# A DiT block on one core: the unused tile in front of the left-hand activations, 64 bytes in place of 192

## The chip, the cores and the metric

The kernel runs on one core of a Trainium2 chip. The metric is the device time of one execution in microseconds; the time before is the median of three runs. The profile is one execution of the same program, recorded instruction by instruction.

## The reference, cut to what matters

One block of a diffusion transformer over 256 latent and 256 context tokens, all in float32:

```
mod = silu(c) @ w_ada + b_ada                      # shift, scale, gate, twice
h   = modulate(rmsnorm(x))                         # latent and context
z   = h @ w_in      # differential attention q k v, MLA compressions, two gates
o_a, o_b = two attentions of 8 heads (latent queries, all keys)
x   = x + g1 * ((sigmoid(ga) * (o_a @ w_o_da) + sigmoid(gb) * (o_b @ w_o_mla)) @ w_out)
x   = x + g2 * ((silu(h2 @ w_gate) * (h2 @ w_up)) @ w_down)   # hidden size 5632
out = rmsnorm(x)                                   # model size 2048
```

The change leaves all of it as it is.

## The kernel before, in words

Activations lie in SBUF with the features on the partitions and the tokens in the free dimension. Every weight matrix is streamed once from HBM, in units of up to 512 KB: `load_w` (L161) puts a unit of 128 x 1024 values into one of five `raw` buffers, and `split_w` makes two parts of it, a rounded part `wh` (ScalarE copy, L169) and the rest `wl` (VectorE subtraction, L170), each with three buffers. The activations are kept as such a pair too. A product is three matmuls: rounded weights with both parts of the activations, and the weights' rest with the rounded activations.

Nearly all matmuls are issued by `Acc.mm` (L155 is the first of a PSUM bank, L157 all others). `GroupT` loads a 128x128 piece of the weights into the array and streams 256 tokens of an activation (gate, up, ga, gb, yab, wo, cq and others). `group_b` does it the other way round: it loads 128 tokens of an activation and streams the weights, 256 columns for dv and 512 for the down projection. A gate or up group is 512 features, 8 units of two k-tiles, 192 matmuls; there are 11 of each, in turn. In groups 2 to 6 a background generator, `gemv` (L495 to L512), multiplies a row of `w_ada` on VectorE into `gacc` at each tick, and after 16 of them its sink issues four matmuls into `gs` (L932 and L933) with 512 columns. The order on TensorE is the program's order; a matmul waits for its unit's split, and the split for its load and for a free buffer.

SBUF tiles come from two stacks. Pools without a side are laid one behind the other from low addresses, pools with `side="right"` from the top downwards. The low stack is `const`, then `stream` (wl, wh, raw), then `apart`, which holds one tile, `gap`, that nothing reads or writes, and then the left-hand pools: kvp, tp, oT, kp, oTbp, qp, yp, xtp, h2p, op, gp and dp. A tile's room is rounded up to 32 bytes in each partition. The program's layout before, in bytes of a partition, with the remainder by 512:

| tiles | first address | remainder |
|---|---|---|
| wl, wh, raw (stream) | 25,120, 37,408, 49,696 (last raw ends at 70,176) | 32 |
| ckvn, x2k (left) | 70,368 | 224 |
| h (left; moving operand of gate and up) | 86,752 and 103,136 | 224 |
| ph, pl (left) | 93,920 and 102,112 | 224 |
| oTa, oTb, cqn, dk, kn (left) | 110,560, 126,944, 143,328, 126,944, 151,520 | 480 |
| hl, hc and mT (right) | 196,576 and 163,808 | 480 |
| hid (right; loaded operand of down) | 130,336 and 175,392 | 288 |

The right-hand pool of the feed-forward part has an unused tile of its own, `hgap`, of 192 bytes, which the change leaves.

Of the kernel before, what the change touches and what calls it, by code (L numbers as in the profile page):

```python
# [11 lines left out]
F32 = mybir.dt.float32  # L12
# [6 lines left out]
P = 128  # L19
# [77 lines left out]
def kernel(  # L97
# [9 lines left out]
    def pool(name, bufs=1, space=None, side=None):  # L107
        st = ExitStack()
        kw = {}
        if space is not None:  # L110
            kw["space"] = space
        if side is not None:
            kw["side"] = side
        pl = st.enter_context(tc.tile_pool(name=name, bufs=bufs, reuse_waits="tile", **kw))
        return pl, st.close
# [5 lines left out]

    apart, _c3 = pool("apart")
    ctx.callback(_c3)
    apart.tile([P, 48], F32, name="gap")
    pacc, _c2 = pool("pacc", space=PSUM)
    ctx.callback(_c2)

# [909 lines left out]
```

## Time and profile before

| | |
|---|---|
| median of three runs | 1593.17 us (1586.82 to 1597.92) |
| the profiled execution | 1590.97 us |
| its span, first to last instruction | 1589.2 us |
| TensorE busy with matmuls | 1536.9 us (97%) |
| VectorE, ScalarE, GpSimd busy | 1015.8, 736.8, 16.1 us |
| read from HBM | 352.37 MB, 223 GB/s over the span |

Busy time of TensorE counts each matmul to its modelled end, and matmuls overlap, so it doesn't say how fast they follow each other. In the chain of waits, a piece such as "PE up L157 x187" is a row of matmuls that follow each other, and its length is the sum of their distances from start to start. Some matmul records are missing from a trace, so a count can be short by a little.

### The profile page before, as it was taken

How to read it: one execution, taken by the hardware profiler on the slowest of the kernel's cores; microseconds unless marked ns; L12 is line 12 of the kernel's file. 1: busy time of each engine (PE TensorE's matmuls, PEld its weight loads, DVE VectorE, ACT ScalarE, POOL GpSimd, SP SyncE). 2: the span in 40 equal slices, each digit the busy share in tenths (PEclk: the TensorE clock that was granted, in tenths of full speed). 3: DMA queues.
4: the chain of work that ended last, by engine and by line, in shares of the span. 5: the costliest groups of instructions: out<-in, count | busy, mean ns of one | idle time of the engine just before them, and what ended most of it. 6: DMA issues, size and time to landing. Idle time of an engine off the chain costs nothing.

```text
span 1589.2 us, 28863 instructions
## 1 busy us (share of the span) xinstructions
PE 1536.9 (97%) x11966; PEld 1443.3 (91%) x11966; DVE 1015.8 (64%) x1360; ACT 736.8 (46%) x1038; POOL 16.1 (1%) x14
## 2 busy tenths in 40 slices
PE   3899999998999999999999999999999999999997
PEld 2678899998899999999999999999999999888886
DVE  5437887787896667677777566767555545455454
ACT  4335455545675444444446444444444444344343
POOL 0000000000000000000000000000000000011010
PEclk9999999999999999999999999999999999999999
DMA  9894653456454787878884668888566656665563
GB/s 369 338 366 161 210 176 111 139 176 202 150 160 162 258 280 259 291 266 296 299 280 148 229 226 300 289 271 280 196 191 196 197 192 220 194 192 197 191 193 120
DMA packets 100595, 356.34 MB, mean 224 GB/s; under 512 B 10993, under 2 KB 13553, under 8 KB 100209
## 3 DMA queue, kind: packets, MB, share of 16 engines
q1 hardware_dynamic: 99600, 351.58, 65.9%
q10 hardware_dynamic: 864, 2.93, 0.5%
q8 instruction: 93, 1.52, 0.4%
q14 instruction: 38, 0.30, 0.1%
HBM read 352.37 MB, written 2.10 MB: 223 GB/s over the span
## 4 chain that ended last, share of the span: by engine, by line
PE 72%; DMA 9%; DVE 6%; issue 1%; ACT 1%; DVEq 0%; POOLq 0%; POOL 0%; ACTq 0%
PE gate L157 15%; PE up L157 15%; PE down L157 15%; DMA raw<-in_w_ada_dram 9%; PE ga L157 4%; PE dv L157 4%; PE gb L157 3%; DVE gacc L507 3%; PE dk L157 2%; DVE wl L170 2%; PE yab L157 2%; PE wo L157 2%; PE dq L157 1%; PE cq L157 1%; PE pt L647 1%
## 5 line engine op out<-in xcount | busy, mean ns | idle before, releaser
L170 DVE TENSOR_TENSOR wl<-raw,wh 128x1024 fp32r<-128x1024 f32 (+1 forms) x453 | 548.9, 1222 | 326.9 <-ACT wh L169 312.6
L169 ACT CAST wh<-raw 128x1024 fp32r<-128x1024 f32 (+1 forms) x453 | 474.9, 1051 | 572.7 <-PE down L157 134.9
L507 DVE SCALAR_TENSOR_TENSOR gacc<-raw,cols,gacc 128x1024 f32<-128x1024 f32 x120 | 154.0, 1283 | 123.5 <-DMA raw<-in_w_ada_dram 123.2
L157 PE MATMUL gate<-h,wh 128*128 128x256 f32 x1386 | 175.9, 277 | 0.0
L157 PE MATMUL up<-h,wh 128*128 128x256 f32 x1386 | 175.8, 277 | 0.0
L157 PE MATMUL down<-wh,hid 128*128 128x512 f32 x696 | 173.3, 389 | 0.0
L157 PEld LDWEIGHTS up<-h,wh 128*128 128x128 f32 x1386 | 166.4, 188 | 0.1
L157 PEld LDWEIGHTS gate<-h,wh 128*128 128x128 f32 x1386 | 166.5, 188 | 0.0
L157 PEld LDWEIGHTS down<-wh,hid 128*128 128x128 f32 x696 | 130.7, 188 | 27.0
L157 PE MATMUL gate<-h,wl 128*128 128x256 f32 x704 | 96.7, 277 | 0.0
L157 PE MATMUL up<-h,wl 128*128 128x256 f32 x704 | 96.7, 277 | 0.0
L157 PE MATMUL down<-wl,hid 128*128 128x512 f32 x352 | 94.6, 389 | 0.0
L157 PEld LDWEIGHTS up<-h,wl 128*128 128x128 f32 x704 | 87.8, 188 | 0.2 <-DVE wl L170 0.2
L157 PEld LDWEIGHTS gate<-h,wl 128*128 128x128 f32 x704 | 87.8, 188 | 0.1
L157 PEld LDWEIGHTS down<-wl,hid 128*128 128x128 f32 x352 | 66.1, 188 | 13.7
L157 PE MATMUL ga<-hl,wh 128*128 128x256 f32 x504 | 65.6, 278 | 0.0
L157 PE MATMUL wo<-mT,wh 128*128 128x256 f32 x504 | 64.2, 278 | 0.0
L157 PE MATMUL gb<-hl,wh 128*128 128x256 f32 x504 | 64.0, 278 | 0.0
L157 PEld LDWEIGHTS ga<-hl,wh 128*128 128x128 f32 x504 | 61.4, 188 | 0.6 <-ACT wh L169 0.4
L157 PEld LDWEIGHTS wo<-mT,wh 128*128 128x128 f32 x504 | 60.6, 188 | 0.4 <-issue 0.4
L157 PEld LDWEIGHTS gb<-hl,wh 128*128 128x128 f32 x504 | 60.7, 188 | 0.0
L408 PE MATMUL pgb<-sraw,c 128*32 128x512 f32 (+1 forms) x288 | 32.8, 597 | 17.4 <-DMA sraw<-in_w_mod_dram 17.4
(334 smaller groups left out, 2316.5 us busy)
## 6 DMA issues: line engine op xcount, KB each, us to landing
raw<-in_w_ada_dram SPq DMA_DIRECT2D x128, 512.0 KB, 4.2
raw<-in_w_in_dram SPq DMA_DIRECT2D x119, 512.0 KB, 4.6
raw<-in_w_ffn_gate_dram SPq DMA_DIRECT2D x88, 512.0 KB, 4.4
raw<-in_w_ffn_up_dram SPq DMA_DIRECT2D x88, 512.0 KB, 4.4
raw<-in_w_ffn_down_dram SPq DMA_DIRECT2D x88, 512.0 KB, 3.6
sraw<-in_w_mod_dram SPq DMA_DIRECT2D x64, 512.0 KB, 8.5
raw<-in_w_out_dram SPq DMA_DIRECT2D x32, 512.0 KB, 5.1
raw<-in_w_o_da_dram SPq DMA_DIRECT2D x16, 512.0 KB, 4.8
```

The source lines that it names most:

```text
L157: nc.tensor.matmul(region, lhsT, rhs, start=False, stop=last, skip_group_check=key != self.lead)
L169: nc.scalar.copy(h, v)
L170: nc.vector.tensor_sub(l, v, h.bitcast(F32))
L408: nc.tensor.matmul(pgb[32 * j : 32 * j + 32, :w], c32[:, kt, :], vs[kt], start=kt < 4, stop=kt >= 12, tile_position=(0, 32 * j))
L507: nc.vector.scalar_tensor_tensor(a, raw, cols[:, kt : kt + 1], a, op0=ALU.mult, op1=ALU.add)
L647: nc.tensor.transpose(pt[:, j * P : (j + 1) * P], a[:, j * P : (j + 1) * P], ident)
```

## The change

The unused tile `gap` gets 16 float32 values in each partition in place of 48, 64 bytes in place of 192.

```diff
     apart, _c3 = pool("apart")
     ctx.callback(_c3)
-    apart.tile([P, 48], F32, name="gap")
+    apart.tile([P, 16], F32, name="gap")
     pacc, _c2 = pool("pacc", space=PSUM)
     ctx.callback(_c2)
```

## Rows read from the trace of the kernel before

**Rows 1.** The page, busy time of each engine.
```profile
PE 1536.9 (97%) x11966; PEld 1443.3 (91%) x11966; DVE 1015.8 (64%) x1360; ACT 736.8 (46%) x1038; POOL 16.1 (1%) x14
```
**Rows 2.** The chain of waits in time, feed-forward part: start us, us, what.
```profile
965.89 21.19 PE up L157 x187
987.65 21.20 PE gate L157 x187
1010.35 22.02 PE up L157 x187
...
1078.19 22.02 PE gate L157 x187
1101.72 21.19 PE up L157 x187
...
1341.20 59.16 PE down L157 x261
```
**Rows 3.** Windows, TensorE: from:to, us, busy (matmuls), granted clock, DMA share, GB/s.
```profile
493.30:542.40 49.10, 49.10 (x419) 1.00 0.75 254
...
629.20:638.30 9.10, 9.10 (x79) 1.00 0.76 245
...
785.30:807.70 22.40, 22.40 (x192) 1.00 0.88 314
...
1009.60:1100.00 90.40, 90.40 (x769) 1.00 0.83 281
1101.10:1340.30 239.20, 239.20 (x2113) 1.00 0.60 196
```
**Rows 4.** The chain of waits in time, other stages.
```profile
215.76 16.84 PE dv L157 x143
...
276.69 21.19 PE dv L157 x187
...
509.38 22.02 PE gb L157 x187
531.99 10.72 PE yab L157 x91
544.06 4.88 PE yab L157 x43
```
**Rows 5.** The timeline at 1008 us, TensorE from gate over gs to up.
```profile
1008.23 0.62 PE L157 MATMUL gate<-h,wl 128*128 128x256 f32 x4
...
1008.68 0.39 PE L932 MATMUL gs<-wh,ones_r 128*128 128x512 f32 x1
...
1009.60 0.28 PE L155 MATMUL up<-h,wh 128*128 128x256 f32 x1
```
**Rows 6.** Groups by line and shape: busy us, mean ns of one, then idle before.
```profile
L170 DVE TENSOR_TENSOR wl<-raw,wh 128x1024 fp32r<-128x1024 f32 x451 | 547.6, 1224 | 324.6 <-ACT wh L169 312.6 <-PE dv L157 6.3 <-PE gs L521 3.0
...
L157 PE MATMUL gate<-h,wh 128*128 128x256 f32 x1386 | 175.9, 277 | 0.0
...
L548 DVE TENSOR_TENSOR pl<-pt,ph 128x512 fp32r<-128x512 f32 x32 | 21.9, 687 | 3.9 <-ACT ph L547 3.5
...
L548 DVE TENSOR_TENSOR hid<-s,hid 128x512 fp32r<-128x512 f32 x22 | 15.1, 688 | 4.8 <-ACT hid L547 4.8
...
L659 PE MATMUL po<-ph,mv 128*128 128x256 f32 x32 | 9.6, 299 | 0.0
...
L548 DVE TENSOR_TENSOR mT<-ga,mT 128x512 fp32r<-128x512 f32 x8 | 5.2, 686 | 0.0
```
**Rows 7.** DMA issues into left-hand tiles: count, KB each, median us to landing.
```profile
x2T<-in_xt_dram SPq DMA_DIRECT2D x4, 512.0 KB, 6.5
...
fgb<-in_final_norm_g_dram ACTq DMA_DIRECT2D x1, 1024.0 KB, 7.5
```
**Rows 8.** The timeline from 128 to 142 us: last modulation matmuls, first temporary.
```profile
128.63 3.64 PE L408 MATMUL pgb<-sraw,c 128*32 128x512 f32 x32
...
141.31 0.44 DVE L555 STREAM_SHUFFLE r<-g 128x256 f32<-128x256 f32 x1
```
**Rows 9.** Windows over other stretches of long spacing, columns as in rows 3.
```profile
215.90:232.40 16.50, 16.50 (x142) 1.00 0.57 171
...
39.30:41.20 1.90, 1.90 (x18) 1.00 1.00 395
...
133.80:148.90 15.10, 15.10 (x130) 1.00 0.35 106
...
856.00:867.30 11.30, 11.30 (x97) 1.00 0.01 1
```

## The prediction
> **What bounds the kernel now.** I read the page's busy shares first, then the chain of waits in order of time, then windows over TensorE's long stretches, and last the groups by line and shape. TensorE is busy 1536.9 of 1589.2 us, VectorE 1015.8, ScalarE 736.8 [rows 1]. The two feed-forward projections, gate and up, fill the span from 855 us to 1340 us and the down projection the rest; in all of it the chain runs on TensorE from group to group with no piece of another engine between them [rows 2]. So what counts is how far one matmul starts behind the one before it, and that can be read from the chain, since a piece of 187 matmuls in sequence lasts 187 spacings.
>
> There are two spacings for the same shape. Most gate and up groups take 21.19 or 21.20 us for 187, 113.3 ns each; four groups in a row, from 1010 to 1100 us, take 22.02 us, 117.8 ns each [rows 2]. The granted clock is 1.00 (the level of 2.4 GHz) in both, so it isn't the clock [rows 3]. The same two spacings are met outside that stage: dv 21.19 us for 187 and 16.84 for 143 (117.8), gb 22.02 for 187, yab 10.72 for 91 (117.8) and 4.88 for 43 (113.5) [rows 4]. The down projection, with 512 columns, takes 59.16 us for 261, 226.7 ns, which is twice 113.3 [rows 2]. The switch comes where another kind of matmul stands between: the gate group that ends at 1008.7 us is followed by four 512-column matmuls into gs, and the up group behind them begins at 117.8 ns [rows 5]; behind the next four gs matmuls, at 1100.2 us, the pieces are short again [rows 2]. No address differs between the gate groups on either side. A spacing, once taken up, is held until the next break.
>
> **The change, part by part.** It removes 128 bytes of a tile that nothing reads or writes: no instruction, no DMA and no wait goes or comes, and the order on every queue stays. What it does is to lower the start of every left-hand tile allocated behind the gap by 128 bytes in each partition. By the positions in the kernel's description, h goes from 224 to 96 past a multiple of 512, and the weights stay at 32: its distance to them goes from 192 to 64. For oTa, oTb, cqn and the dk and kn tiles the distance goes from 448 to 320. Between two left-hand tiles nothing changes, and right-hand tiles (hl, hc, mT, hid) keep theirs.
>
> Step 1, VectorE and ScalarE: VectorE's 128x512 subtraction takes 688 ns into hid (288 past a multiple of 512), 686 into mT (480) and 687 into pl (224) [rows 6]. Three positions, one duration within 2 ns; 2 ns on the 32 writes of pl are under 0.1 us either way, beside TensorE's work. The costly split, 1224 ns times 451, touches only the weights' pool, which doesn't move [rows 6]. I take 0.
>
> Step 2, DMAs: the weights' buffers don't move. The loads into moved tiles are four of x2T, 6.5 us from issue to landing, and one of final_g, 7.5 us [rows 7]. Each x2T load lies beside a w_out group of TensorE and only has to land before that group's end. If that cover were gone, the four would cost 26 us; nothing in the change takes it. I take 0.
>
> Step 3, buffer reuse: the moved tiles overlap slightly other parts of the closed right-hand pools. The modulation weights (sraw) are last read at 132.3 us and the first left-hand temporary (r) is written at 141.3 us [rows 8], so a wait that comes or goes there is over 9 us early. I take 0; the bounds are nothing gained and, with that cover gone, 9 us once.
>
> Step 4, TensorE, the only step with a real unknown: does the distance between the streamed operand and the loaded one set the spacing? The rows of before contain the new distance already. In dv the streamed operand is wh (32) and the loaded one hl or hc (480), so the streamed one lies 64 past the other, counted round 512, just as h will lie to wh in gate and up. There the two spacings are 113.3 and 117.8 ns, no other [rows 4]. And at the distance of 448 (gb, and yab) the same two are seen [rows 4], as at 192 in gate and up [rows 2]. So I expect the same two spacings afterwards, and the break, not the address, to choose which. The cost of the step is then what the choice falls on.
>
> The price of the choice: 117.8 less 113.3 is 4.5 ns a matmul. The stretches of long spacing that last over some 140 matmuls and the one of 79 at 629 us hold 419, 79, 192, 769 and, in dv, 142 matmuls; twelve short ones, of 18 to 130, hold 569 more (97 of them at 856 us) [rows 3, 9]: 2,170 in all, so about 9.7 us of this execution. If all of them went, 1590.97 us would become 1581.3. Should the one long stretch of 2,113 matmuls from 1101 us [rows 3] begin at the other spacing, it would cost 2,113 times 4.5 ns, 9.5 us. The three runs of before lie 11.1 us apart (1586.82 to 1597.92), which is what one or two such stretches are worth. I take the expected change of step 4 as zero, with 8 us to either side.
>
> Sum: 0 + 0 + 0 + 0 on the profiled execution of 1590.97 us (span 1589.2 and 1.8 around it). That execution is 2.2 us under the median of the runs shown, 1593.17. I put the forecast between them: 1592 us, no change, with a range of its own from 1584 to 1600.
>
> **The rivals.** About 1% is what a measurement of this kernel can tell from no change: under 1577.2 or over 1609.1 us.
>
> A, slower: at the distances 64 and 320 the left-hand stages fall into the long spacing at each restart. Place: gate and up first, 4,224 matmuls of which 769 and 97 have it already; 3,358 times 4.5 ns is 15.1 us. yab has 768, some 100 long already: 3.0 us. cq and the latent-attention projections have some 300 left: 1.3 us. Together 19.4 us, 1610 us. It decides from the point where more than 4,000 matmuls take up the long spacing. A third, longer one is not excluded by the few hundred dv matmuls: 6 ns beyond the short one in place of 4.5 would make it 1616. The far end is the row of po, which streams ph at 299 ns a matmul against gate's 277 [rows 6]; 22 ns on 4,224 matmuls would be 93 us and 1684, but those stand in short runs behind waits, so it is no estimate. For A: nothing else that could set the rhythm changes here, and both spacings are a coin's toss now, so a bias could be large. Against: dv held the short one for 187 in a row at that distance.
>
> B, slightly faster: the new distance rids the left-hand stages of the long spacing. 769 and 97 in gate and up, about 100 in yab and 180 in the latent-attention part are 1,146; times 4.5 ns is 5.2 us, 1586 us. Against it: dv at that distance shows the long spacing too.
>
> C, faster: the short spacing itself becomes shorter in gate and up. It needs 3.3 ns on each of 4,224 to pass 1577. No row shows a spacing under 113.3 for 256 columns, and down has it to the digit for twice the columns at another distance (the streamed wh 256 from hid), so nothing here supports it. As a mechanism: the two operands now hold each other up a little even in the short spacing, and the new distance would spare them that; priced from the rows it gives 1577 at the 3.3 ns that it needs. The Trainium skill speaks for it: its page "TensorE: Matmul & The Clock Gate", section "Back-to-back issue gap", gives the columns divided by 2.4 GHz and 2.5 ns more, 109.2 ns for 256 columns. By that figure 4.1 ns on 4,224 matmuls would be an estimated 17 us and 1574; this trace doesn't agree with it at any of its distances.
>
> D, that the change doesn't do what it says: a tile's room could be rounded up so that nothing moves. The raw buffers end at 70,176 and the first left-hand tile begins at 70,368, exactly 192 later, so the gap is laid out at its size; 64 will be, too. Its time would be that of the forecast.
>
> **How the numbers follow.** Forecast with D 0.55, A 0.24, B 0.11, C 0.10. Faster by over 1% is C alone, 0.10. Within 1% are the forecast and B, 0.66. Slower by over 1% is A, 0.24; it sits on the limit, and its chance holds the longer spacings that the rows don't exclude. The range takes the forecast, B, and A up to 1613, and stops below at 1581, the floor of step 4; what is left out is C and the far part of A.
>
> **What would show each step right or wrong.** Right: the chain's pieces of 187 in gate and up again last 21.19 or 22.02 us, in a mixture, with the switches at gs or other breaks; down stays at 59.16 us for 261; the 128x512 subtractions stay at 686 to 688 ns. A is shown by gate and up at 22.02 us throughout or at a new, longer piece; B by no 22.02 in gate, up and yab but still in ga, gb or wo; C by pieces under 21.1 us. The prediction is wrong if gate and up show any third length, or if the total moves by over 1% while the spacings stay, for then the time has gone somewhere that I costed at nothing.

## The result and the profile after

The changed kernel takes 1609.34 us in the median (1602.33 to 1611.17, 8 runs), the kernel before in the same sessions 1592.77 us (1586.82 to 1597.92, 8 runs). The ratio is 1.0097 with a 95% interval of 1.008 to 1.0114: slower, by 16.6 us, inside the stated range and 17 us over the forecast. The profiled execution took 1610.15 us, its span is 1608.4.

The page after, busy time of each engine, as [rows 1]:

```profile
PE 1558.2 (97%) x11966; PEld 1466.6 (91%) x11966; DVE 1017.4 (63%) x1360; ACT 737.4 (46%) x1038; POOL 16.1 (1%) x14
```

The counts are the same and the order of the instructions is the same on every engine. TensorE has gained 21.3 us of busy time, VectorE 1.6 and ScalarE 0.6. The chain of waits in time, feed-forward part, as [rows 2]:

```profile
906.15 22.02 PE gate L157 x187
...
996.60 22.03 PE gate L157 x187
1020.15 22.02 PE up L157 x187
...
1111.53 22.02 PE up L157 x187
...
1337.66 22.02 PE up L157 x187
...
1420.23 59.16 PE down L157 x261
```

Every gate and up group is at the long spacing now, 22.02 us for 187 or 117.8 ns a matmul, ahead of the first gs break (the group at 996.60), between the two, and behind the second (1111.53); a gs break is the four matmuls into gs that stand between two groups. The down projection has kept its 59.16 us. No third length appears. Windows place the time; these are the kernel before, from the first gate matmul to the last up matmul and from there to the end (columns as in [rows 3]):

```profile
855.30:1340.30 485.00, 484.97 (x4234) 1.00 0.68 226
1340.30:1589.20 248.90, 239.58 (x1058) 0.99 0.58 186
```

and these are the same two stretches of the kernel after:

```profile
859.80:1359.60 499.80, 499.78 (x4234) 1.00 0.65 220
1359.70:1608.40 248.70, 239.37 (x1056) 0.99 0.57 186
```

Gate and up went from 485.0 to 499.8 us, 14.8 of the 19.2 us between the two spans, at the same granted clock of 1.00. They start 4.5 us later, which is what the stages ahead of them lost in this execution; what follows is equal within 0.2 us. Counted in the trace, matmuls of gate and up that start 116 to 119 ns behind the one before were 869 before and are 4,211 now; 3,342 more at 4.44 ns (22.02 less 21.19 us, by 187) are 14.8 us.

The VectorE work that the forecast costed at nothing did cost nothing. Groups by line and shape after, as [rows 6]:

```profile
L170 DVE TENSOR_TENSOR wl<-raw,wh 128x1024 fp32r<-128x1024 f32 x451 | 547.9, 1224 | 345.3 <-ACT wh L169 331.9 <-PE dv L157 10.8 <-PE ga L157 0.7
...
L548 DVE TENSOR_TENSOR pl<-pt,ph 128x512 fp32r<-128x512 f32 x32 | 21.9, 686 | 3.9 <-ACT ph L547 3.5
...
L548 DVE TENSOR_TENSOR mT<-ga,mT 128x512 fp32r<-128x512 f32 x8 | 5.2, 685 | 0.0
```

pl has moved by 128 bytes and its subtraction takes 686 ns, where it took 687.

### The profile page after: what moved, and what is told of

Its sections match the earlier page's. It is cut to its first block, busy times and chain, and to the rows that moved or that the text cites. A ratio compares the mean times of both kernels' runs of the same rounds, so it can differ in the third digit from the quotient of the medians.

```text
span 1608.4 us, 28863 instructions
## 1 busy us (share of the span) xinstructions
PE 1558.2 (97%) x11966; PEld 1466.6 (91%) x11966; DVE 1017.4 (63%) x1360; ACT 737.4 (46%) x1038; POOL 16.1 (1%) x14
## 4 chain that ended last, share of the span: by engine, by line
PE 82%; DMA 3%; DVE 3%; issue 1%; ACT 1%; POOLq 0%; POOL 0%; DVEq 0%; ACTq 0%
PE up L157 15%; PE gate L157 15%; PE down L157 15%; PE ga L157 6%; PE gb L157 5%; PE yab L157 5%; PE dv L157 4%; DMA raw<-in_w_ada_dram 3%; PE dk L157 3%; PE wo L157 2%; PE dq L157 2%; PE cq L157 1%; DVE wl L170 1%; PE pt L647 1%; DVE gacc L507 1%
## 5 line engine op out<-in xcount | busy, mean ns | idle before, releaser
L157 PE MATMUL gate<-h,wh 128*128 128x256 f32 x1386 | 180.6, 279 | 0.0
L157 PE MATMUL up<-h,wh 128*128 128x256 f32 x1386 | 180.6, 279 | 0.0
L157 PEld LDWEIGHTS up<-h,wh 128*128 128x128 f32 x1386 | 170.9, 188 | 0.1
L157 PEld LDWEIGHTS gate<-h,wh 128*128 128x128 f32 x1386 | 170.9, 188 | 0.0
```

The costliest lines, as they stand in the source:

```text
L157: nc.tensor.matmul(region, lhsT, rhs, start=False, stop=last, skip_group_check=key != self.lead)
```

## The experiments

The theories: 1, the distance between h and the weights decides the spacing of gate and up; 2, the position of h by itself does; 3, the spacing is a draw, and h's place has no part in it. Distances are h's address less the weights': 192 before, 64 after. In the table further down they are counted round 256 bytes, for the reason that stands behind it.

**h_back: the change, with h put back.**

```diff
     h2p, close_h2 = pool("h2p")
+    h2p.tile([P, 32], F32, name="h2gap")
```

on top of the changed kernel.

> The gap stays at 64 bytes, and an unused tile of 128 bytes in h2p, ahead of h, puts h and what lies above it back to their places of before (h at 224 past a multiple of 512, 192 from the weights); ckvn, oTa, oTb, cqn and the attention tiles stay 128 lower. If the place of h decides gate and up (theories 1 and 2): pieces of 187 at 21.19 us for most groups again, and 1594 to 1600 us. If the spacing is a draw that h has no part in (theory 3): gate and up stay at 22.02 us, about 1609 us.

1593.05 us (10 runs), a ratio to before of 0.9982 (0.9956 to 1.0007). The chain in time:

```profile
945.95 21.19 PE gate L157 x187
...
1012.16 22.02 PE up L157 x187
...
1103.53 21.19 PE up L157 x187
```

Gate and up are as before to the stretch: long between the gs breaks (868 matmuls, 869 before), short else. The left-hand tiles ahead of h stay 128 bytes lower, and the slowdown is gone. So the rest of the change is worth nothing that these times can tell, though its traces show it in other products (below).

**h_only: the kernel before, with h alone moved.**

```diff
     h2p, close_h2 = pool("h2p")
+    h2p.tile([P, 96], F32, name="h2gap")
```

> The gap stays at 192 bytes as before the change, and an unused tile of 384 bytes in h2p moves h alone (and what lies above it) to 96 past a multiple of 512, where the change put it. Theories 1 and 2: gate and up at 22.02 us for 187 in all or nearly all groups, 1603 to 1609 us. Theory 3: a mixture as before, about 1593 us.

1605.44 us (9 runs), ratio 1.0058 (1.0032 to 1.0085); the kernel before had come out wide beside it, 1589.04 to 1605.22. The chain in time:

```profile
947.73 22.02 PE gate L157 x187
...
1016.49 22.03 PE up L157 x187
...
1107.86 22.03 PE up L157 x187
```

All 4,214 counted matmuls are long, and no other left-hand tile that a big product streams has moved. Theory 3 falls: the place of h has a part in it.

**w_near: h where it was, the weights 128 bytes higher.** The gap has 64 bytes, and

```diff
     const, _c0 = pool("const")
     ctx.callback(_c0)
+    const.tile([P, 32], F32, name="cgap")
```

> The gap has 64 bytes and an unused tile of 128 bytes at the start of the constants moves the weights up by 128 (to 160 past a multiple of 512), so that every left-hand tile lies where it lay before the change, but 64 from the weights. Theory 1 (the distance between streamed and loaded operand decides): gate and up at 22.02 us, about 1603 to 1612 us. Theory 2 (the streamed operand's own position decides): gate and up mostly at 21.19 us, about 1593 us. hl comes to lie 320 from the weights and may move ga and gb too.

1618.30 us (4 runs), ratio 1.0150 (1.0096 to 1.0203). The chain in time:

```profile
952.01 22.02 PE gate L158 x187
...
1020.79 22.02 PE up L158 x187
...
1361.04 60.90 PE down L158 x261
```

h's own address is that of before, and gate and up are long throughout: theory 2 falls, the distance counts. No run moves h and the weights together by the same amount, so a part of the weights' own place is not tested by itself; the short pieces of this run further down show that this place alone doesn't force the long spacing. The weights' move also changed their distance to the right-hand tiles, hl, hc, mT and hid, and the down projection shows it: 60.90 us for 261 in place of 59.16, 6.7 ns a matmul. From the last up matmul to the end the run takes 256.0 us and the change 249.0, which is 7.0 of the 7.6 us between their spans (1616.0 and 1608.4).

**gap0: no gap.** The changed kernel without the unused tile:

```diff
-    apart.tile([P, 16], F32, name="gap")
```

> No gap at all: h at 32 past a multiple of 512, as the weights, a distance of 0. Theory 1: a third state of gate and up, either all short or all long; if the distance matters by 256 or 512, 0 is as unlike 192 as can be, and I expect the long spacing, 22.02 us for 187 and about 1609 us or more. Theory 2 says the same of position 32 and doesn't differ here. Theory 3: a mixture, 1587 to 1610 us.

1615.41 us (4 runs), ratio 1.0138 (1.0096 to 1.0181). The chain in time:

```profile
947.84 22.44 PE gate L156 x187
...
1110.94 22.44 PE up L156 x187
```

A third spacing, 120.0 ns, in all groups. That the long one would come was wrong; that 0 is worse than 192 was right.

**The other distances, h alone moved.** Each is the kernel before with an unused tile of so many float32 values in h2p, as in h_only: h256 has 16, h448 64, h224 8, h128 112, h160 120, h32 24, h96 40.

> The kernel before with 64 unused bytes in h2p ahead of h: h lies 256 from the weights, everything else below it as before. If the distance counts by 256 (theory 1a), this is the case of no gap: gate and up at 22.44 us for 187 in every group, 120 ns a matmul, some 24 us over before. If it counts by 512 (theory 1b), 256 is a place of its own, not 22.44; as the down projection lies 256 from hid at 226.7 ns for 512 columns, I would then expect 21.19.

> The same with 256 unused bytes: h lies 448 from the weights, as hl does. Theory 1a: as 192, that is gate and up at 21.19 us with the stretch of 22.02 between the two gs breaks. Theory 1b: another picture, for instance 21.19 throughout or 22.02 throughout.

> The same with 32 unused bytes: h lies 224 from the weights and starts at a multiple of 64, where all tiles so far start at 32 past one. If what counts is the stretch of 64 bytes that an address lies in (theory 1), 224 falls between 192 and 256: a mixture or 22.02 throughout. If a start inside a 64-byte stretch costs a little by itself, the pieces come out under 21.19 us for 187.

> The same with 448 unused bytes: h lies 128 from the weights counted by 512. Theory 1 has no row for it yet; by 256 it is as far from 0 as can be, so 21.19 us for 187 in all groups and about 4 us under before if a larger distance is better, or 22.02 throughout if 128 is half the way to a second collision, as the down projection of the run with moved weights suggests, which took 60.90 us for 261 at 384.

> The kernel before with 480 unused bytes in h2p, so that h lies 160 from the weights by 256, between 128 (22.19 us) and 192 (21.19 and 22.02). Theory 1, with 224 at 22.12 on the other side: between the two, about 22.0 to 22.1 us for 187 in all groups, about 1607 us; 192 then stands alone among the distances tried.

> The kernel before with 96 unused bytes in h2p: h lies 32 from the weights by 256. Theory 1: between 0 (22.44 us) and 64 (22.02), about 22.2 us for 187, 1611 us.

> The kernel before with 160 unused bytes in h2p: h lies 96 from the weights by 256, between 64 (22.02 us) and 128 (22.19). Theory 1: 22.0 to 22.2 us for 187, 1608 us; no distance but 192 then holds the short spacing.

Measured, with one execution each for these seven (the piece of 187 in the second half of the stage; for 192 and 64 the kernels before and after):

| h to the weights, by 256 | run | 187 matmuls | one time, or median |
|---|---|---|---|
| 0 | gap0, h256 | 22.44 us | 1615.41, 1614.03 |
| 32 | h32 | 21.82 | 1601.24 |
| 64 | after, h_only | 22.02 | 1609.34, 1605.44 |
| 96 | h96 | 22.44 | 1615.37 |
| 128 | h128 | 22.19 | 1609.11 |
| 160 | h160 | 21.94, from the first gs break 22.19 | 1607.58 |
| 192 | before, h448 | 21.19 or 22.02 | 1592.77, 1593.62 |
| 224 | h224 | 22.12 | 1610.18 |

The lines behind the two pairs of equal distance, h256 first (gap0 stands above), then h448:

```profile
947.66 22.44 PE gate L157 x187
```

```profile
946.57 21.19 PE gate L157 x187
...
1013.03 22.02 PE up L157 x187
...
1104.40 21.19 PE up L157 x187
```

Distances of 0 and 256 agree, and 192 and 448: the count by 256 (theory 1a) holds for gate and up and that by 512 doesn't. The expectation for h32, 22.2 us, was wrong, and so was that for h96, 22.0 to 22.2; those for h128 and h224 named 21.19, 22.02 or a mixture, and 22.19 and 22.12 came. The curve is not smooth. What it has in common with the expectations is that no distance but 192 shows 21.19.

**A second product in the same traces.** yab loads the weights and streams an activation (oTa or oTb), as gate and up do. Its tiles lie 448 from the weights in the kernel before, 320 with a gap of 64 bytes and 256 without a gap, which is 192, 64 and 0 by 256. The same piece in h448, in the changed kernel and in gap0, in this order:

```profile
595.72 10.31 PE yab L157 x91
...
600.26 10.72 PE yab L157 x91
...
597.99 10.91 PE yab L156 x91
```

These are 113.3, 117.8 and 119.9 ns a matmul, the three spacings of gate and up at the same distances. Of its 768 matmuls, 101 to 105 are long in each of the twelve traces in which yab lies as in the kernel before, and 663 or 665 in each of the five with 64 (after, h_back, gs8_64, gs6_64, w_near); in gap0 726 are at 120 ns. In w_near its tiles have the addresses of before, so here too the distance counts.

But 64 doesn't shut the short spacing out of every product. In those five traces yab keeps 93 to 96 short matmuls, and in w_near, where hl lies 320 from the weights as well, most of the first ga group and the gb and yab groups behind it are short, 416 matmuls:

```profile
494.11 14.62 PE ga L158 x129
509.30 21.19 PE gb L158 x187
531.06 10.31 PE yab L158 x91
```

Whether this is the 320 in place of gate's 64, or the place in the program, no run tells.

**What sets one spacing or the other at 192.** gs8 and gs6 are the kernel before with a longer gs break, gs8_64 and gs6_64 the changed kernel with the same; the second pass writes the same result again.

```diff
-            nc.tensor.matmul(ps, ones_r, h[:, i, :], start=True, stop=False)
-            nc.tensor.matmul(ps, ones_r, l[:, i, :], start=False, stop=True)
+            for _ in range(2 if i == 0 else 1):
+                nc.tensor.matmul(ps, ones_r, h[:, i, :], start=True, stop=False)
+                nc.tensor.matmul(ps, ones_r, l[:, i, :], start=False, stop=True)
```

That is gs6; gs8 has `True` for `i == 0`.

> The kernel before (192 bytes) with each pair of gs matmuls issued twice, so that a gs break holds eight matmuls of 512 columns in place of four; the second pair writes the same result again. Theory 4 (at 192 the break sets which spacing follows): the pattern in gate and up changes, so that the four groups between the breaks, at 22.02 us before, take 21.19, or others take 22.02; 1587 to 1606 us. Theory 5 (the stretch belongs to something else that happens from 1010 to 1100 us, such as the transfers): the same four groups stay at 22.02.

> The same with only the first pair of each gs break issued twice, six matmuls in place of four. Theory 4: another pattern still, and where two breaks of equal length flip the spacing twice, the groups after the second break are as those ahead of the first. Theory 5: 22.02 us in the same four groups only.

> The changed kernel (64 bytes) with eight gs matmuls in a break. If 64 leaves no short spacing whatever the break (theory 1): 22.02 us in all gate and up groups, about 1610 us. If 64 only has the two spacings the other way round at the states that the breaks lead to, some groups come out at 21.19.

gs8 took 1585.04 us and gs6 1586.87, once each, where the kernel before took 1592.03 beside them; gs8_64 took 1609.52. In gs8 and gs6 all gate and up groups were short, with the same transfers from 1010 to 1100 us, so these by themselves don't make the stretch long: theory 5 falls. gs8_64 was long throughout. But the chain of gs6,

```profile
1009.18 21.19 PE up L157 x187
...
1097.62 21.19 PE up L157 x187
```

was not that of the very same program when it was run again to be timed:

> The kernel before (192 bytes) with six gs matmuls in a break, now timed against it. If the spacing after a break follows the program (theory 4), gate and up are short again in every group: 866 matmuls of long spacing fewer, 3.9 us, less 2 times 2 matmuls of 0.23 us, 0.9 us: some 3 us faster than before, 0.2%, with other stages adding or taking a few. If the single look was chance, no difference.

```profile
966.61 21.19 PE up L157 x187
...
1011.67 22.02 PE up L157 x187
...
1103.52 22.02 PE up L157 x187
```

Here the first gs break ended the short spacing and the second didn't bring it back. The 12 runs went from 1583.64 to 1603.51 us, median 1589.38; the ratio to before is 0.9994 (0.9976 to 1.0013), no difference. So at 192 the program doesn't fix what follows a break: theory 4 in that form falls too. This is shown with six gs matmuls. With four, the three traces at 192 (before, h_back, h448) show the same pattern, and that it is a draw there as well is not shown; the spread of the kernel before in one group of runs, 1589.04 to 1605.22 us, would fit it. No version here beats the kernel before by what can be measured.

> The changed kernel (64 bytes) with six gs matmuls in a break, the length that kept all groups short at 192. Theory 1: 22.02 us in all gate and up groups, about 1609 us. If some break does lead to the short spacing at 64 too, pieces of 21.19 appear.

1607.98 us, once. The chain after the first gs break:

```profile
1040.12 22.03 PE gate L157 x187
...
1109.34 22.02 PE up L157 x187
```

All 4,212 are long. In five profiles at a distance of 64 (after, h_only, w_near, gs8_64, gs6_64), behind gs breaks of four, six and eight matmuls, gate and up never kept the short spacing.

## Why the prediction was wrong

Steps 1 to 3 were right as far as the rows go: the subtraction into pl takes 686 ns, no instruction changed its order, the x2T loads land after 6.1 us in place of 6.5, and the first dq matmul, behind the place of step 3, starts at 150.37 us before and 150.45 after. The view was right as well: the chain's pieces of 187 showed the change in one line, and the price of 4.5 ns a matmul was the measured one, 4.44.

The step that failed is step 4: "I expect the same two spacings afterwards, and the break, not the address, to choose which." It rested on dv as a row that already held the new distance. But dv loads the activations and streams the weights, and its 64 was counted as streamed less loaded. Gate and up do it the other way round, and at 64 they show the long spacing alone, which h_only and w_near put down to the distance. So there the address chose, and not the break: 14.8 us that step 4 took as zero. And dv's rows were no measurement of gate at 64. Counted as activations less weights, dv before is at 192, the case of gate before; yet in w_near, where that count gives 64, dv keeps a short piece too:

```profile
216.37 16.23 PE dv L158 x143
277.50 22.02 PE dv L158 x187
```

(16.23 us for 143 is 113.5 ns). So neither way of counting carries over from one product to another, and the row should not have been used as a proof.

The half of step 4 that stands is that at 192 the spacing behind a break can be either, as gs6 and gs6_timed show. The forecast carried that over from one distance to another, and from dv to gate and up. Nor was yab's mixture at 448 a row for its new distance: it came out about 102 long matmuls at 448 and about 665 at 320 each time.

Rival A was what happened, down to the sum: 15.1 us in gate and up forecast, 14.8 measured; 1610 us in total, 1609.34 measured. That the two totals agree so well is in part luck, for ahead of gate and up the long spacing came otherwise than the rival says. yab has 105 long matmuls before and 665 after, 560 at 4.44 ns or 2.5 us against the 3.0 of the rival. But dv, dq and dk, of which no streamed or loaded tile moved, became longer too: 273 long matmuls before, 1,079 after. That is no chance of one execution. The four runs with a gap of 64 bytes and the weights in place (after, h_back, gs8_64, gs6_64) have 1,079 to 1,238, the twelve with the gap of 192 have 157 to 641; what carries the spacing over to these products is not shown. Little of it reaches the time: gate starts at 856.5 to 859.6 us in those four and at 850.9 to 857.7 in the twelve, and h_back, which has all of it, is not slower than before. The error was in the chances: A had 0.24, since the dv rows were counted against it. The rows for it, two spacings at equal clock in one group of instructions, were already a sign that something other than the count of columns sets the pace.

B, C and D fall: gate and up show no piece of 187 under 22.02 us after, and putting h back by 128 bytes brings the old pieces back, so it had moved.

The Trainium skill, in "TensorE: Matmul & The Clock Gate", section "Step-by-step: what each phase is for", step 1, says that the engine has two independent read ports and that loading the next tile's weights takes no read bandwidth from the running matmul. That passage says nothing of addresses; here the same matmuls with the same loads follow each other at 113.3 to 120.0 ns by the distance of their operands. Whether the two reads slow each other, against that rule, no run here shows.

Not settled is what in the memory does it. That the two reads meet in one part of the memory when their addresses agree by 256 bytes would fit 0 and 256 at 22.44 us, but 96 takes 22.44 as well and 32 less than 64. Behind equal sums lie unequal patterns: in gap0 nearly all single spacings are 120 ns, in h96 they go from 115 to 125. Nothing here shows the reads themselves.

## What to carry to other kernels

Where a chain runs from matmul to matmul, divide its pieces by their counts: two lengths for one shape at one clock were the sign here that something outside the instruction sets the pace, and the addresses of the operands are among the candidates. A move of one tile by 128 bytes was worth 3% of a stage here, and an unused tile ahead of that operand alone tests it with everything else in place. Don't take the same distance in another product, with loaded and streamed operand exchanged, as a measurement of yours.

## What the runs showed that was not expected

In gate and up, the spacing of matmuls with a loaded 128x128 piece and 256 streamed float32 columns depends on the distance of the two tiles, counted by 256 bytes, from 21.19 us to 22.44 us for 187, and not smoothly; yab shows three of these spacings at the same distances. At 192 two spacings exist, one is taken up at a break and then kept for up to 2,113 matmuls, and it can differ between executions of one program. The 12 runs of gs6_timed go from 1583.64 to 1603.51 us; between the two traces of this program, gs6 and gs6_timed, lie 15.2 us, of which 12.7 are gate and up. The 512-column stream of the down projection, with its roles exchanged, has such a dependence as well: 59.16 us for 261 where the streamed weights lie 256 from hid, 60.90 where they lie 384 from it.
